# Reciprocal square roots on VectorE in 8 steps for one column and 11 for several, in place of 12

## The chip, the cores and the metric

The kernel runs on one core of one Trainium2 chip. The metric is device time in microseconds (us) of the whole program. Below, PE is TensorE (matmuls; PEld are its weight loads), DVE is VectorE, ACT is ScalarE, POOL is GpSimd, and SP is SyncE, which issues most DMAs. P is 128, the number of partitions; "128x3" is a tile of 128 partitions with 3 elements each, which the texts call 3 columns.

## The reference

One step of a diffusion backbone of width 1024 with one layer: 128 context tokens and 1024 latent tokens, nine blocks of 128. Each layer has an attention head group (8 query heads and 2 key heads of 64) and a bidirectional mLSTM head group (4 heads of 128) side by side, one output projection, and a SwiGLU FFN of hidden width 2816. What matters for this change is that a root-mean-square norm stands at five places of the layer:

```python
def rmsnorm(x, w):
    xf = x.astype(F32)
    y = xf * lax.rsqrt(jnp.mean(xf * xf, axis=-1, keepdims=True) + EPS)
    return (y * w.astype(F32)).astype(x.dtype)

def trunk_layer(x, mods, ...):
    sh1, sc1, g1, sh2, sc2, g2 = mods
    h = rmsnorm(x, norm1_w) * (1 + sc1) + sh1
    aq, ak, av, mq, mk, mv, mo, mg = jnp.split(h @ w_in, SPLIT_POINTS, axis=-1)
    aq = rmsnorm(aq.reshape(B, T, N_Q_HEADS, HEAD_DIM), q_norm_w)
    ak = rmsnorm(ak.reshape(B, T, N_KV_HEADS, HEAD_DIM), k_norm_w)
    ...
    attn_o = attention(aq, keys, vals)
    hm, st_f, st_b = mlstm_bidir(...)
    hm = rmsnorm(hm.transpose(0, 2, 1, 3), mlstm_norm_w.reshape(MLSTM_HEADS, MLSTM_DV))
    hm = (hm.reshape(B, T, MLSTM_WIDTH) * jax.nn.sigmoid(mo.astype(F32))).astype(x.dtype)
    mix = jnp.concatenate([attn_o, hm], axis=-1) @ w_out
    x = x + g1 * mix
    h2 = rmsnorm(x, norm2_w) * (1 + sc2) + sh2
    x = x + g2 * swiglu(h2, w_gu, w_down)
    return x, ak, av, st_f, st_b
```

and once more over the result (`y_prompt = rmsnorm(xp, final_norm_w)`, and the same for the samples).

## The kernel before, in words

The nine token blocks are held in three column blocks (c) of three blocks each (CB is 3, CT is 384 tokens). The program runs in these stages, by the trace's time: loads, the adaLN modulations, the norm of x and its transposes (to about 100 us); the input projection, the q and k norms with rotary and the mLSTM scans (100 to 490); the context tokens' output projection (`prefill`) beside the last mLSTM head and the first attention scores (490 to 610); attention with the output projection and the FFN of earlier column blocks woven beside it (610 to 980); the last column block's norm and the start of the seven-product FFN stage (980 to 1060); that stage's gate and up products (1060 to 1460); and the last outputs.

Products of f32 quality are made of two parts: a weight block is loaded as `raw` (or straight as `whi`), and its high part and remainder are multiplied separately. In the last FFN stage, `weights6` makes the two halves of each operand: ACT casts the scaled high part (L1637, tile A), DVE the remainder (L1638), and the PE lines L1651 to L1653 use them.

The function the change touches is `rsqrt` (L130). From a sum of squares `ss` in n columns it makes v = ss * inv + plus, a first guess of the reciprocal root out of the bits of v by integer arithmetic (a shift, L137, and a multiply and add, L138), and three Newton steps of three DVE instructions each (L140, L141, L142). Every instruction reads what the one ahead of it wrote. Its tiles are rv (v), rh (the shifted bits), ry (the guess) and rt.

It is called 23 times:

- `normalise` (L401), three times with 3 columns: ssx, the sums of squares of x that ACT made (L400), at 10, 15 and 42 us.
- `norm_rope` (L718), eight times with 2 to 16 columns: the q and k norms, between 73 and 174 us.
- the `tail` of `head_mlstm` (L980), six times: three times 9 columns (305, 412, 509 us) and three times 3 columns (519, 532, 559 us); POOL multiplies the head's output hm by the root (L981).
- `stats` (L1445), six times. Three times with one column in `end` of `prefill`, one for each block (575, 577, 583 us): ACT squares a block (L1444), and `norm2` on ACT reads the root (L1460) and goes on to transposes on PE and to the scaled result `fl` (L1470). Three times with 3 columns (721, 941, 1020 us), the last in `finish`, where DVE writes the result (L1531).

What sets the order on each engine is a scheduler: the program's tasks are given in the written order with priorities (`hot(n)` raises it for a few), and the Tile framework sets the instructions of each engine's queue by simulating the program with its own costs. One instruction fewer can so move others on every engine. Each engine runs its queue in order, and an instruction whose operand isn't ready holds up everything behind it.

Names in the other lines of the prediction: L232 sums squares of weight blocks of w_in (iraw); L488 copies the modulation strips (part) out of a PSUM bank for the PE line L497; L615 and L616 are steps of the mLSTM gates (gc, gd), each with an ACT table load; L192 to L208 make a power of two (pv) that PE spreads; L960 makes nu in the mLSTM and L957 reads sd and va; L1134 to L1139 are the softmax of attention (S, pr, ph, pl).

Of the kernel before, what the change touches and what calls it, by code (L numbers as in the profile page):

```python
# [12 lines left out]
I32 = mybir.dt.int32  # L13
AF = mybir.ActivationFunctionType
ALU = mybir.AluOpType
# [4 lines left out]
P = 128  # L20
# [30 lines left out]
def hybrid_step(ctx: ExitStack, tc: tile.TileContext, I: dict, O: dict):  # L51
# [3 lines left out]
    dve = nc.vector  # L55
# [7 lines left out]
    def nm(s):  # L63
        uid[0] += 1
        return f"{s}_{uid[0]}"
# [64 lines left out]
    def rsqrt(tp, ss, n, inv, cap=16, plus=EPS):  # L130

        v = tp.tile([P, cap], F32, name=nm("rv"), tag="rv", bufs=2)[:, :n]
        y = tp.tile([P, cap], F32, name=nm("ry"), tag="ry", bufs=2)[:, :n]
        t = tp.tile([P, cap], F32, name=nm("rt"), tag="rt", bufs=2)[:, :n]
        h = tp.tile([P, cap], I32, name=nm("rh"), tag="rh", bufs=2)[:, :n]
        dve.tensor_scalar(out=v, in0=ss, scalar1=inv, scalar2=plus, op0=ALU.mult, op1=ALU.add)
        dve.tensor_scalar(out=h, in0=v.bitcast(I32), scalar1=1, scalar2=None, op0=ALU.logical_shift_right)  # L137
        dve.tensor_scalar(out=y.bitcast(I32), in0=h, scalar1=-1, scalar2=0x5F3759DF, op0=ALU.mult, op1=ALU.add)  # L138
        for _ in range(3):
            dve.tensor_tensor(out=t, in0=y, in1=y, op=ALU.mult)  # L140
            dve.scalar_tensor_tensor(out=t, in0=t, scalar=-0.5, in1=v, op0=ALU.mult, op1=ALU.mult)  # L141
            dve.scalar_tensor_tensor(out=y, in0=t, scalar=1.5, in1=y, op0=ALU.add, op1=ALU.mult)  # L142
        return y

# [216 lines left out]
    for n in (1, 4):  # L361
        dve.tensor_scalar(out=bcol[:, n * KD : (n + 1) * KD], in0=bcol[:, n * KD : (n + 1) * KD],
                          scalar1=1.0, scalar2=None, op0=ALU.add)
# [31 lines left out]
    def normalise(c):  # L395

        ssx = p0.tile([P, CB], F32, name=f"ssx{c}")
        for i in range(CB):
            jk = p0.tile([P, D], BF16, name=nm("jk"), tag="jk", bufs=2)
            act(jk, x3[c][:, i], AF.Square, accum_out=ssx[:, i : i + 1])  # L400
        rs = rsqrt(p0, ssx, CB, 1.0 / D)  # L401
        for i in range(CB):
            dve.tensor_scalar(out=x3[c][:, i], in0=x3[c][:, i], scalar1=rs[:, i : i + 1], scalar2=None, op0=ALU.mult)
# [305 lines left out]
    def norm_rope(qp, cc, ss, x, nb, nh, w, rb):  # L709

        skip = nb - (rb[1] - rb[0])
        n = nb * nh
        sq = qp.tile([P, 1024], F32, name=nm("nr0"), tag="nr0", bufs=1)[:, 0 : n * HD].rearrange("p (h d) -> p h d", d=HD)
        xf = x.rearrange("p b h d -> p (b h) d")
        act(sq, xf, AF.Square)
        ssum = qp.tile([P, 16], F32, name=nm("nrs"), tag="nrs", bufs=2)[:, :n]
        dve.tensor_reduce(out=ssum, in_=sq, axis=AX.X, op=ALU.add)
        r = rsqrt(qp, ssum, n, 1.0 / HD)  # L718
        pool.tensor_tensor(out=xf, in0=xf, in1=bc(r, 2, [P, n, HD]), op=ALU.mult)
        if skip:  # L720
            pool.tensor_tensor(out=xf[:, 0 : skip * nh], in0=xf[:, 0 : skip * nh], in1=bc(w, 1, [P, skip * nh, HD]), op=ALU.mult)
        if rb[1] == rb[0]:
            return
        t2 = qp.tile([P, 1024], F32, name=nm("nr1"), tag="nr0", bufs=1)[:, 0 : n * HD].rearrange("p (b h d) -> p b h d", b=nb, d=HD)
        for i, b in enumerate(range(rb[0], rb[1])):
            s4 = ss[:, b, :].rearrange("p (a f) -> p a f", a=2)
            x4 = x[:, skip + i].rearrange("p h (a f) -> p h a f", a=2)
            t4 = t2[:, skip + i].rearrange("p h (a f) -> p h a f", a=2)
            for f in range(2):
                dve.tensor_tensor(  # L730
                    out=t4[:, :, :, 16 * f : 16 * f + 16],
                    in0=x4[:, :, :, 16 - 16 * f : 32 - 16 * f],
                    in1=bc(s4[:, :, 16 * f : 16 * f + 16], 1, [P, nh, 2, 16]),
                    op=ALU.mult)
        m = nb - skip
        pool.tensor_tensor(out=x[:, skip:], in0=x[:, skip:], in1=bc(cc[:, rb[0] : rb[1], :], 2, [P, m, nh, HD]), op=ALU.mult)
        dve.tensor_tensor(out=x[:, skip:], in0=x[:, skip:], in1=t2[:, skip:], op=ALU.add)
# [155 lines left out]
    def head_mlstm(h, st):  # L893
# [44 lines left out]
        for b in range(NB):  # L938
# [36 lines left out]
            if b in ends:  # L975
                def tail(b=b):
                    b0 = ends[b]
                    n = b + 1 - b0
                    v = hm[:, b0 : b + 1, :]
                    r = rsqrt(mlp, ssh[:, b0 : b + 1], n, 1.0 / P)  # L980
                    pool.tensor_tensor(out=v, in0=v, in1=bc(r, 2, [P, n, P]), op=ALU.mult)  # L981
                    for c in range(b0 // CB, b // CB + 1):
                        if c == 0:
                            dma(hm_d[0][:, h * P : (h + 1) * P].rearrange("(b p) n -> p b n", p=P), hm[:, 0:CB, :])
                        else:
                            (pool.dma_start if alone else dma)(hm_d[c][:, h], hm[:, c * CB : (c + 1) * CB, :].rearrange("p b n -> p (b n)"))

                tails.append(tail)
                if h != NH - 2:
                    tails.pop()()  # L990
# [1000 lines left out]
```

## Time and profile before

| what | value |
|---|---|
| timed runs | 1489.94, 1495.63, 1496.03 us; median 1495.63 |
| profiled execution | 1491.52 us, of which its span is 1489.8 us |
| granted TensorE clock, mean | 0.989 |
| PE, DVE, ACT, POOL busy | 1406.6, 1102.7, 875.8, 218.7 us |
| DVE instructions on the page | 2233 |
| DMA | 206.46 MB, mean 139 GB/s |

The span is the time between the first and the last instruction of the trace; the time of an execution has a little around it. A row of the timeline gives the start, the length, the engine, the line, the operation, what is written and read, and in brackets how long the engine had been idle and what ended that. A row of a group gives how many instructions there were, the shortest, median and longest in ns, the first and last start in us, and the forms. A row of waits gives the total us, the number of times, and the longest.

### The profile page before, as it was taken

What the parts mean: (1) busy time and instruction counts of PE and PEld (TensorE: products, weight loads), DVE (VectorE), ACT (ScalarE), POOL (GpSimd) and SP (SyncE); (2) the same over time, 40 slices, a digit from 0 to 9 for tenths busy, and PEclk for the clock granted to TensorE, in tenths of its full rate; (3) what the DMA queues carried; (4) which work ended last, traced back from release to release, by engine and by line L of the source; (5) the groups of instructions that cost most, each with busy time, mean ns of one, the idle gap of its engine ahead of it and who ended that gap; (6) DMA issues with size and microseconds to landing.
All of it is one profiled execution on the core that took longest, in us unless ns stands there. A gap on an engine that the chain in (4) does not pass through costs nothing.

```text
span 1489.8 us, 22801 instructions
## 1 busy us (share of the span) xinstructions
PE 1406.6 (94%) x8285; PEld 986.0 (66%) x8285; DVE 1102.7 (74%) x2233; ACT 875.8 (59%) x1619; POOL 218.7 (15%) x310
## 2 busy tenths in 40 slices
PE   6789999998899889999999999999999999999996
PEld 3634667766677657888999997985645654654552
DVE  4978556775777978667687768798976867786667
ACT  5854476866857745563766754859642642463254
POOL 0113422232222434420100010010000000000000
PEclk9999999999999989999999999999999999999998
DMA  9565323643558966675757765469231321232112
GB/s 368 174 193 197 96 75 65 145 90 74 92 108 166 198 200 163 157 212 159 212 162 167 188 138 155 142 209 348 88 105 43 112 74 43 72 116 67 45 43 85
DMA packets 256166, 206.46 MB, mean 139 GB/s; under 512 B 167022, under 2 KB 208198, under 8 KB 256054
## 3 DMA queue, kind: packets, MB, share of 16 engines
q1 hardware_dynamic: 253054, 199.00, 48.2%
q10 hardware_dynamic: 2872, 5.62, 1.2%
q8 instruction: 65, 1.06, 0.3%
q14 instruction: 47, 0.39, 0.1%
q0 software_dynamic: 128, 0.39, 0.1%
HBM read 153.38 MB, written 13.26 MB: 112 GB/s over the span
## 4 chain that ended last, share of the span: by engine, by line
PE 51%; DVE 6%; DMA 5%; ACT 4%; issue 2%; POOL 1%; SPq 0%; ACTq 0%; DVEq 0%; POOLq 0%
PE mm L1651 5%; PE mm L1653 5%; PE mm L1652 5%; PE mm L1482 3%; PE mm L1481 3%; PE mm L1483 3%; PE mm L1735 3%; PE mm L1736 3%; PE mm L1737 3%; PE mm L1220 2%; PE S L1132 2%; PE mm L1221 2%; PE mm L1222 2%; PE mm L1256 1%; PE mm L1258 1%
## 5 line engine op out<-in xcount | busy, mean ns | idle before, releaser
L1652 PE MATMUL mm<-Bt,A 128*128 128x384 f16 x616 | 200.8, 326 | 0.0
L1651 PE MATMUL mm<-Bt,A 128*128 128x384 f16 x616 | 198.4, 326 | 1.5 <-DVE u L1670 1.2
L1653 PE MATMUL mm<-Bt,A 128*128 128x384 f16 x616 | 197.4, 326 | 2.3 <-DVE A L1638 2.2
L146 DVE TENSOR_TENSOR wlo<-raw,whi 128x1024 fp32r<-128x1024 f32 (+1 forms) x78 | 95.1, 1221 | 38.6 <-ACT whi L175 35.2
L1139 DVE SCALAR_TENSOR_TENSOR pl<-pr,st,ph 128x1152 f16<-128x1152 f32 (+1 forms) x72 | 96.1, 1335 | 36.9 <-ACT ph L1138 36.9
L175 ACT CAST whi<-raw 128x1024 fp32r<-128x1024 f32 (+1 forms) x78 | 79.7, 1027 | 70.7 <-PE mm L1221 26.2
L1483 PE MATMUL mm<-aTh,wlo 128*128 128x384 f32 x352 | 119.1, 339 | 0.5 <-DVE wlo L146 0.5
L1481 PE MATMUL mm<-aTh,whi 128*128 128x384 f32 x352 | 119.2, 339 | 0.0
L1482 PE MATMUL mm<-aTl,whi 128*128 128x384 f32 x352 | 118.9, 338 | 0.0
L1135 ACT ACTIVATE pr<-S,st 128x1152 f32<-128x1152 f32 (+1 forms) x72 | 81.5, 1132 | 56.9 <-DVE st L1134 55.6
L1134 DVE TENSOR_REDUCE st<-S 128x1 f32<-128x1152 f32 (+1 forms) x72 | 88.9, 1235 | 25.4 <-PE S L1132 25.3
L530 PE MATMUL wi<-headw,hT 128*128 128x384 f16 x288 | 94.5, 328 | 1.2 <-ACT th L820 1.2
L531 PE MATMUL wi<-headw,hT 128*128 128x384 f16 x288 | 94.5, 328 | 0.0
L532 PE MATMUL wi<-headw,hT 128*128 128x384 f16 x288 | 94.3, 328 | 0.0
L1138 ACT ACTIVATE ph<-pr,st 128x1152 f16<-128x1152 f32 (+1 forms) x72 | 83.8, 1164 | 13.9 <-DVE st L1137 5.3
L1132 PE MATMUL S<-kst,qT 128*128 128x384 f32 (+1 forms) x400 | 87.6, 349 | 4.0 <-ACT pr L1135 4.0
L1653 PEld LDWEIGHTS <-A 128*128 128x128 f16 x616 | 60.3, 98 | 43.4 <-DVE A L1638 3.8
L1652 PEld LDWEIGHTS <-A 128*128 128x128 f16 x616 | 60.3, 98 | 42.0 <-issue 2.2
L1651 PEld LDWEIGHTS <-A 128*128 128x128 f16 x616 | 60.3, 98 | 40.4 <-ACT A L1637 0.4
L146 POOL TENSOR_TENSOR hl<-tn,hl 128x384 fp32r<-128x384 f32 x22 | 30.7, 1396 | 309.0 <-ACT hl L1504 285.3
L1132 PEld LDWEIGHTS S<-kst,qT 128*128 128x128 f32 x400 | 69.4, 189 | 7.8 <-ACT pr L1135 5.4
L1637 ACT ACTIVATE A<-S,six 128x1024 f16<-128x1024 f32 x44 | 48.9, 1142 | 38.7 <-DVE S L1632 19.4
(478 smaller groups left out, 3718.9 us busy)
## 6 DMA issues: line engine op xcount, KB each, us to landing
raw<-in_w_gu_dram SPq DMA_DIRECT2D x88, 512.0 KB, 3.4
raw<-in_w_down_dram SPq DMA_DIRECT2D x42, 512.0 KB, 3.8
a<-in_w_ada_dram SPq DMA_DIRECT2D x24, 512.0 KB, 6.5
whi<-in_w_down_dram SPq DMA_DIRECT2D x22, 512.0 KB, 8.7
iraw<-in_w_in_dram SPq DMA_DIRECT2D x32, 256.0 KB, 3.4
x<-in_x_sample_dram SPq DMA_DIRECT2D x11, 512.0 KB, 5.9
raw<-in_w_out_dram SPq DMA_DIRECT2D x10, 512.0 KB, 3.7
aw<-in_w_ada_dram SPq DMA_DIRECT2D x8, 512.0 KB, 6.0
```

Source lines behind the costliest of these rows:

```text
L146: (dve if eng == "dve" else pool).tensor_tensor(out=out, in0=full, in1=hi, op=ALU.subtract)
L530: mm(ps[:, :n], ah, wh[:, k % 2, c0 : c0 + n], start=(k == 0), stop=False)
L531: mm(ps[:, :n], ah, wl[:, k % 2, c0 : c0 + n], start=False, stop=False)
L532: mm(ps[:, :n], al, wh[:, k % 2, c0 : c0 + n], start=False, stop=(k == KD - 1))
L1132: mm(S[:, n, 0:w], qT[:, h, :], kst[kv][:, t, c0 + n * w : c0 + (n + 1) * w], start=(t == 0), stop=(t == 1))
L1139: dve.scalar_tensor_tensor(out=plv, in0=prv, scalar=st[:, 3:4], in1=phv, op0=ALU.mult, op1=ALU.subtract)
L1481: mm(ps, wh[:, k, :], th[:, k, :], start=(k == 0), stop=False)
L1482: mm(ps, wh[:, k, :], tl[:, k, :], start=False, stop=False)
L1483: mm(ps, wl[:, k, :], th[:, k, :], start=False, stop=(k == KD - 1))
L1651: mm(ps, wh[:, k], bt[:, 0, k], start=first and k == 0, stop=False, skip_group_check=True)
L1652: mm(ps, wh[:, k], bt[:, 1, k], start=False, stop=False, skip_group_check=True)
L1653: mm(ps, wl[:, k], bt[:, 0, k], start=False, stop=k == 3, skip_group_check=True)
```

## The change

Two things are done with `rsqrt`. First, v is kept as -v/2: the factor -0.5 goes into the scale and the addend of the first instruction, so no later step needs it, and the first guess is made from the bits of that in one instruction in place of two. The bits of -v/2 read as an integer, times -0.5 and plus a constant, are the guess; the tile rh goes. That makes 11 instructions out of 12. Second, for a single column the two multiplications y * y * v of a Newton step are one instruction, in which y stands as the per-column scalar operand: 8 instructions out of 12. For several columns the second multiplication is a plain one of two tensors.

```diff
         t = tp.tile([P, cap], F32, name=nm("rt"), tag="rt", bufs=2)[:, :n]
-        h = tp.tile([P, cap], I32, name=nm("rh"), tag="rh", bufs=2)[:, :n]
-        dve.tensor_scalar(out=v, in0=ss, scalar1=inv, scalar2=plus, op0=ALU.mult, op1=ALU.add)
-        dve.tensor_scalar(out=h, in0=v.bitcast(I32), scalar1=1, scalar2=None, op0=ALU.logical_shift_right)
-        dve.tensor_scalar(out=y.bitcast(I32), in0=h, scalar1=-1, scalar2=0x5F3759DF, op0=ALU.mult, op1=ALU.add)
+        dve.tensor_scalar(out=v, in0=ss, scalar1=-0.5 * inv, scalar2=-0.5 * plus, op0=ALU.mult, op1=ALU.add)
+        dve.tensor_scalar(out=y.bitcast(I32), in0=v.bitcast(I32), scalar1=-0.5, scalar2=0x5F3759DF - 2 ** 30 - 2 ** 22, op0=ALU.mult, op1=ALU.add)
         for _ in range(3):
-            dve.tensor_tensor(out=t, in0=y, in1=y, op=ALU.mult)
-            dve.scalar_tensor_tensor(out=t, in0=t, scalar=-0.5, in1=v, op0=ALU.mult, op1=ALU.mult)
+            if n == 1:
+                dve.scalar_tensor_tensor(out=t, in0=y, scalar=y, in1=v, op0=ALU.mult, op1=ALU.mult)
+            else:
+                dve.tensor_tensor(out=t, in0=y, in1=y, op=ALU.mult)
+                dve.tensor_tensor(out=t, in0=t, in1=v, op=ALU.mult)
             dve.scalar_tensor_tensor(out=y, in0=t, scalar=1.5, in1=y, op0=ALU.add, op1=ALU.mult)
         return y
```

PE, ACT, POOL and SP have as many instructions as before, but the scheduler puts some of them in another order. In the changed kernel lines from 143 on have a number one higher. Three places follow; rows are an instruction's line, operation, and what it writes and reads.

ACT where the mLSTM gates' steps (gc, gd) meet the modulation strips (part), at 96 to 102 us of the trace; before:

```order
L232 ACTIVATE jkw,isc_1224<-iraw_1073 128x512
L615 ACT_TABLE_LOAD
L615 ACTIVATE gc<-gb 128x128
L232 ACTIVATE jkw,isc_1224<-iraw_1073 128x512
L488 COPY part_1190<-mm_962 128x512
L616 ACT_TABLE_LOAD
L616 ACTIVATE gd<-gc 128x128
L775 ACTIVATE qraw_1310<-wi_1084,isc_736 128x512
```

and now:

```order
L233 ACTIVATE jkw,isc_1214<-iraw_1067 128x512
L616 ACT_TABLE_LOAD
L616 ACTIVATE gc<-gb 128x128
L233 ACTIVATE jkw,isc_1214<-iraw_1067 128x512
L617 ACT_TABLE_LOAD
L617 ACTIVATE gd<-gc 128x128
L489 COPY part_1182<-mm_956 128x512
L776 ACTIVATE qraw_1298<-wi_1078,isc_730 128x512
```

The copy to part now stands behind the second table load and gd.

DVE in `end` of `prefill`, at the single-column calls (574 to 584 us); before:

```order
L136 TENSOR_SCALAR rv_7074<-s_1414_7071 128x1
L137 TENSOR_SCALAR rh_7077<-rv_7074 128x1
L138 TENSOR_SCALAR ry_7075<-rh_7077 128x1
L140 TENSOR_TENSOR rt_7076<-ry_7075 128x1
L1134 TENSOR_REDUCE st_7191<-S_7192 128x1
L141 SCALAR_TENSOR_TENSOR rt_7076<-rt_7076,rv_7074 128x1
L1209 TENSOR_TENSOR t_1434_7173<-mm_7160,gl_6966 128x512
L136 TENSOR_SCALAR rv_7143<-s_1427_7140 128x1
L142 SCALAR_TENSOR_TENSOR ry_7075<-rt_7076,ry_7075 128x1
L146 TENSOR_TENSOR mx_7176<-mm_7177,mx_7176 128x512
```

and now:

```order
L135 TENSOR_SCALAR rv_7040<-s_1397_7037 128x1
L136 TENSOR_SCALAR ry_7041<-rv_7040 128x1
L139 SCALAR_TENSOR_TENSOR rt_7042<-ry_7041,rv_7040 128x1
L143 SCALAR_TENSOR_TENSOR ry_7041<-rt_7042,ry_7041 128x1
L147 TENSOR_TENSOR mx_7132<-mm_7133,mx_7132 128x512
```

The softmax's reduction (L1134) and the gating of the next block (L1209), which stood between the first call's steps, now stand behind its first Newton step, and the remainder mx (L146), which stood last here, directly follows that step.

ACT at the start of the last FFN stage (1012 to 1018 us): the squares of the last norm (L1444) and the casts of A (L1637); before:

```order
L1444 ACTIVATE jk_11524,s_2272_11523<-x1a 128x1024
L1637 ACTIVATE A_11492<-S_11484,six 128x2x512
L1637 ACTIVATE A_11495<-S_11484,six 128x2x512
L1444 ACTIVATE jk_11526,s_2272_11523<-x1a 128x1024
L1637 ACTIVATE A_11498<-raw_11482,six 128x512
L1444 ACTIVATE jk_11528,s_2272_11523<-x1a 128x1024
```

and now:

```order
L1445 ACTIVATE jk_11471,s_2250_11470<-x1a 128x1024
L1445 ACTIVATE jk_11473,s_2250_11470<-x1a 128x1024
L1638 ACTIVATE A_11439<-S_11431,six 128x2x512
L1638 ACTIVATE A_11442<-S_11431,six 128x2x512
L1445 ACTIVATE jk_11475,s_2250_11470<-x1a 128x1024
L1638 ACTIVATE A_11445<-raw_11429,six 128x512
```

The second square moved ahead of the two casts. On SP, nearby, loads of w_gu (`raw`) and of w_down (`whi`) change places.

## The prediction

> **What bounds the kernel now.** I read the page first (busy time, then the chain that ended last), then a table of stages, then the waits of TensorE (PE) in the stages where it idles. Section 1 and the first line of section 4 of the page:
>
> ```profile
> PE 1406.6 (94%) x8285; PEld 986.0 (66%) x8285; DVE 1102.7 (74%) x2233; ACT 875.8 (59%) x1619; POOL 218.7 (15%) x310
> ...
> PE 51%; DVE 6%; DMA 5%; ACT 4%; issue 2%; POOL 1%; SPq 0%; ACTq 0%; DVEq 0%; POOLq 0%
> ```
>
> PE is busy 1406.6 us of a span of 1489.8, so everything that is not matmul can give back at most 83 us. VectorE (DVE), on which the change lies, holds 6% of the chain. Where PE idles is told by stage (columns: stretch, its length, then busy us and instructions of PE, PEld, DVE, ACT, POOL, the granted clock, the DMA share, GB/s):
>
> ```profile
> 0.00:100.00 100.00, 73.39 (x520) 46.28 (x521) 70.66 (x244) 66.01 (x145) 12.54 (x19) 0.97 0.77 255
> 100.00:490.00 390.00, 373.93 (x2457) 257.71 (x2458) 273.00 (x706) 258.30 (x636) 114.00 (x213) 0.99 0.51 115
> 490.00:610.00 120.00, 101.99 (x577) 78.47 (x577) 99.03 (x258) 69.22 (x151) 50.63 (x50) 0.96 0.65 171
> 610.00:980.00 370.00, 365.26 (x2012) 330.95 (x2011) 274.11 (x409) 238.57 (x353) 38.56 (x28) 1.00 0.64 171
> 980.00:1060.00 80.00, 76.48 (x430) 48.28 (x430) 71.49 (x123) 59.00 (x94) 2.98 (x1) 1.00 0.73 260
> 1060.00:1460.00 400.00, 399.73 (x2224) 217.41 (x2222) 290.47 (x430) 170.36 (x209) 0.00 (x0) 1.00 0.22 72
> ```
>
> From 1060 to 1460 PE idles 0.27 us: nothing on DVE pays there. What can pay lies in the front (26.6 us idle to 100), in 490 to 610 (18.0), and in 980 to 1060 (3.5). The 16.1 us of 100 to 490 are spread over 390.
>
> **The change part by part.** First, how many steps go. The first integer step ran once per call, 23 times:
>
> ```profile
> L137 DVE TENSOR_SCALAR rh<-rv x23: 142/170/2109, 10.5 to 1021.6; 128x3 int32<-128x3 int32 x9, 128x16 int32<-128x16 int32 x4, 128x8 int32<-128x8 int32 x3, 128x9 int32<-128x9 int32 x3
> ```
>
> The 19 forms listed all have several columns; of the four not listed, one has two columns (the first of eight calls of norm_rope) and three have one (stats in prefill's end). So 20 calls lose one step and three lose four: 32 instructions. What a step is worth depends on what stands behind it (start, length):
>
> ```profile
> 11.45 0.16 DVE L140 TENSOR_TENSOR rt<-ry 128x3 f32<-128x3 f32 x1
> 11.64 0.16 DVE L141 SCALAR_TENSOR_TENSOR rt<-rt,rv 128x3 f32<-128x3 f32 x1
> 11.72 0.20 DVE L351 COPY bcol<-mm 128x48 f32<-128x48 f32 x1
> 11.92 0.15 DVE L142 SCALAR_TENSOR_TENSOR ry<-rt,ry 128x3 f32<-128x3 f32 x1
> ```
>
> L141 reads what L140 wrote and starts 0.19 us after it; the copy at 11.72, which needs neither, starts 0.08 after L141. A step on the path is thus worth 0.195 us, one whose gap other work fills some 0.07. The change holds 32 x 0.07 = 2.2 us of DVE throughput, and 32 x 0.195 = 6.2 us if every step is on the path that ends last. That is the scale: at most 0.4% of the time.
>
> The Trainium skill, in "VectorE: DVE Perf Modes", The DRAIN you can't avoid, has a DVE instruction wait until the pipe of the one before is empty, with the semaphore costing nothing extra. By it an independent step would cost its whole 0.16 us too, and the bound on throughput would be 32 x 0.16 = 5.1 us in place of 2.2; the copy at 11.72, begun inside L141's 0.16 us, disagrees, and I go by the row.
>
> *Front, three calls at 10, 15 and 42 us: 0.* The third is the only one near PE's idle time:
>
> ```profile
> 41.13 1.06 ACT L400 ACTIVATE jk<-x 128x1024 bf16<-128x1024 f32 x1 [0.73 <-DMA x<-in_x_sample_dram]
> 42.31 0.17 DVE L136 TENSOR_SCALAR rv<-ssx 128x3 f32<-128x3 f32 x1 [1.26 <-ACT jk L400]
> 42.39 0.13 DVE L192 TENSOR_SCALAR pv<-pv 1x1 f32<-1x1 f32 x1
> 43.05 0.37 PE L208 MATMUL mm<-pv,one 1*128 1x2 f32 x1 [2.31 <-DVE pv L195]
> ```
>
> PE waits for pv, which is queued behind rv, and rv waits for a transfer of x. The step removed follows rv, and pv's steps already run in its gap. Whatever the normalised rows win before 96 us is given back to the next transfer that ScalarE (ACT) waits 3.08 us for, the first line here:
>
> ```profile
> 96.47 0.63 ACT L232 ACTIVATE jkw<-iraw 128x512 bf16<-128x512 f32 x1 [3.08 <-DMA iraw<-in_w_in_dram]
> 97.21 1.28 ACT L615 ACT_TABLE_LOAD   x1
> 99.34 0.56 ACT L488 COPY part<-mm 128x512 f32<-128x512 f32 x1
> 99.92 1.28 ACT L616 ACT_TABLE_LOAD   x1
> 99.95 1.02 PE L497 MATMUL mm<-part,strip_sel 128*2 128x512 f32 x2 [2.11 <-ACT part L488]
> 101.21 0.31 ACT L616 ACTIVATE gd<-gc 128x128 f32<-128x128 f32 x1
> ```
>
> The cover is that transfer; were it gone, the front's three steps would give 3 x 0.195 = 0.6.
>
> *ACT's order at 97 to 102 us: +1.5.* In the new order the table load (1.28) and gd (0.31) stand ahead of the copy to part: 1.59 us later for part, for which PE already waited 2.11 with nothing else to run. Queued behind it are qraw and ACT's evacuations. Bounds: 0 if part's matmuls move behind other work that is ready, 1.6 if PE only waits longer; as PE had nothing ready at 97.8, I take 1.5. The 32 fewer steps don't do this; the scheduler's new order does.
>
> *Normalising of the mLSTM heads, 305 to 560 us: -0.3.* Where GpSimd (POOL) runs a tensor operation, an integer step can sit out its whole length:
>
> ```profile
> 518.89 2.12 POOL L981 TENSOR_TENSOR hm<-hm,ry 128x1152 f32<-128x1152 f32 x1 [0.31 <-DVE rv L136]
> 518.92 2.11 DVE L137 TENSOR_SCALAR rh<-rv 128x3 int32<-128x3 int32 x1
> 522.43 0.71 PE L957 MATMUL wi<-va,sd 128*128 128x129 f32 x4 [1.50 <-DVE nu L960]
> ```
>
> Nu, for which PE waits 1.50 us, stood in DVE's queue behind that step. The step left in its place has the same operand kinds and may sit out the same 2.1 us, so the gain lies between 1.5 (it no longer meets L981) and -0.6 (it meets it a step earlier, for a like stall of some 2.1 where PE has only 1.5 in hand). One dependent step, and a little for the others, is 0.3.
>
> *The three single-column calls, 574 to 584 us: -0.4.* Four steps fewer each, 0.8 us in a row, and other work between:
>
> ```profile
> 579.55 1.29 POOL L1210 TENSOR_TENSOR x1a<-x1a,t 128x512 f32<-128x512 f32 x1 [0.95 <-DVE rt L140]
> 579.58 1.27 DVE L141 SCALAR_TENSOR_TENSOR rt<-rt,rv 128x1 f32<-128x1 f32 x1
> 580.93 1.04 ACT L1444 ACTIVATE jk<-x1a 128x1024 bf16<-128x1024 f32 x1
> 581.97 1.32 ACT L1460 ACTIVATE t<-x1a,ry 128x512 f32<-128x512 f32 x2
> 586.51 1.17 PE L1256 MATMUL mm<-whi,mx 128*128 128x512 f32 x4 [2.08 <-DVE fl L1470]
> ```
>
> A step with two tensors sat 1.27 us beside GpSimd's 1.29. The roots' reader is L1460 on ACT, queued directly behind a square (L1444) of 1.04 us that doesn't wait for any root; then come transposes, L1470 and PE. So the gain is cut to what ACT's queue passes on. Upper bound: PE's whole wait for L1470, 2.08 us. Lower: the three new steps read a per-column operand, and the nearest row of such a read is
>
> ```profile
> L1752 DVE TENSOR_SCALAR lq<-st x6: 206/214/215, 1461.9 to 1483.6; 128x1 f32<-128x1 f32 x6
> ```
>
> 0.214 against 0.15 to 0.16 for the steps above, 0.06 more; nine of them make 0.5 us lost if nothing else is passed on. I take a half step per removed one at one call, 4 x 0.195 / 2 = 0.4.
>
> *ACT and SP at 1010 to 1024 us: +0.5.* In the new order a second square (L1444) stands ahead of the two casts of A:
>
> ```profile
> 1012.76 1.04 ACT L1444 ACTIVATE jk<-x1a 128x1024 bf16<-128x1024 f32 x1
> 1013.80 2.17 ACT L1637 ACTIVATE A<-S,six 128x1024 f16<-128x1024 f32 x2
> 1014.96 2.48 DVE L1638 SCALAR_TENSOR_TENSOR A<-S,six,A 128x1024 f16<-128x1024 f32 x2 [3.67 <-ACT A L1637]
> ...
> PE mm L1653 <- DVE A L1638: 2.2, 3, 1.1
> ```
>
> The casts come 1.04 later (1.23 with the 0.19 that reads the sum), and PE waited 2.2 us for their remainders already. Bounds 0 (matmuls of the pair before still fill it) and 1.2; I take 0.5. SP's loads change order too, with the DMA share at 0.73; at nothing here, and a rival below.
>
> *The rest: 0.* The q and k norms between 73 and 174 us and the calls at 720 and 941 lie beside PE work (3.3% and less idle from 610 to 980); uncovered, their 10 steps are 2.0 us.
>
> Sum: 0 + 1.5 - 0.3 - 0.4 + 0.5 + 0 = +1.3 us. The profiled run took 1491.52 (span 1489.8 and 1.7 around it), so 1492.8. The three timed runs are 1489.94, 1495.63 and 1496.03 (median 1495.63): the profiled one lies near their fastest, and with it the four have a mean of 1493.3. The shift on that mean is 1494.6; I say **1494.5**.
>
> **The rivals.** About 0.5%, 7.5 us, is what a measurement of this kernel can tell from no change.
>
> *Every step on the path* (12%): 1493.3 - 6.2 = 1487, and with the L1470 and nu waits gone as well (2.1 + 1.5) 1483.5. For it: every step waits for the one before, and DVE is 89% busy in 980 to 1060 (71.5 of 80). Against it: DVE's 6% of the chain, and the roots' readers stand behind ACT's queue or a transfer.
>
> *Late weights* (13%): slower. In the new order of SP's queue, loads of w_gu and w_down change places in the stage from 980 to 1060, where the DMA share is 0.73.
>
> ```profile
> raw<-in_w_gu_dram SPq DMA_DIRECT2D x88, 512.0 KB, 3.4
> ...
> whi<-in_w_down_dram SPq DMA_DIRECT2D x22, 512.0 KB, 8.7
> ```
>
> A w_gu block behind one w_down load comes 3.4 to 8.7 us later. From the point where that passes the slack ahead of L1637, PE stands still for it, since each pair's products need its A: 1493.3 + 1.3 + 8.7 = 1503.3 at the full price, 1498 at the lower. Against it: with that share PE idles only 3.5 of these 80 us, and none of the waits there is for a transfer of w_gu.
>
> *The order gives nothing and takes nothing* (part of my own case's chance): part's matmuls fill other gaps and the rest cancels: 1493.3, within 0.5%. That the change doesn't do what it says, 12 steps still, gives the same.
>
> **How the numbers follow.** My forecast with the absorbed case has 75%, its own range 1490 to 1498. All steps on the path have 12%, late weights 13%. Only the full prices of the rivals leave the band of 0.5% around 1495.63 (1488.2 to 1503.1), so half of each counts: 6% faster, 6.5% slower. The order moves on every engine, so effects beyond my list are likely and of either sign; they take 9% to the fast side, where the fastest run shown, 1489.9, is already near the band's end, and 3.5% to the slow side. Faster 0.15, same 0.75, slower 0.10. Range 1486 to 1502.5: all but the extremes of either rival, and the bounds (+1.6 + 0.6 + 0.5 + 1.2 up, 0 - 1.5 - 2.1 - 0.6 - 2.0 down from 1493.3) lie inside.
>
> **What would show it.** DVE's count falls by 32, to 2201 in the profile's counting, and its busy time by 4 to 8 us (stalls included). PE's wait for part grows from 2.11 to 3.6. The wait for L1470 shrinks by under 1 us; the stall beside L981 moves to the new integer step. The 1060 to 1460 stretch stays at 400 us. I am wrong if PE's idle time of a stage falls by over 3 us, or if a wait for raw or whi appears in 980 to 1060.

## The result

The change made the kernel slower by half a per cent: 1499.05 us in the median of 17 runs (1496.83 to 1503.89), against 1491.06 us for 17 runs of the kernel before (1489.40 to 1496.99). The ratio is 1.0052 with a 95% interval of 1.0043 to 1.0061. The forecast was "no change" at 1494.5, a sum of +1.3 us on a base of 1493.3. Measured, the change costs 8.0 us, six times that sum. The time lies in the range that I gave, which was as wide as it was for the rivals' sake; that says nothing for the sum.

The page of the changed kernel, busy time and the head of the chain:

```profile
PE 1411.4 (94%) x8285; PEld 990.3 (66%) x8285; DVE 1097.0 (73%) x2201; ACT 875.1 (58%) x1619; POOL 227.1 (15%) x310
...
PE 48%; DVE 8%; ACT 5%; DMA 5%; issue 2%; POOL 0%; SPq 0%; ACTq 0%; DVEq 0%; POOLq 0%
```

DVE did what the change says: 32 instructions fewer (2233 to 2201) and 5.7 us less busy. PE ran the same 8285 matmuls, but was busy 4.8 us longer (1406.6 to 1411.4). The span grew by 7.3 us (1489.8 to 1497.1), so PE's idle time grew by only 2.5. The same matmuls were busy longer, and the granted clock was lower in two places. One is the first 100 us, with PE busy 73.39 us at a clock of 0.97 before and 76.09 at 0.90 after. This is not what makes the difference: the kernel before has 76.14 us at 0.93 there in a second profile, which took 1490.26 us. The other place is 500 to 610 us. Before (columns as in the prediction: PE, PEld, DVE, ACT, POOL busy, granted clock, DMA share, GB/s):

```profile
500.00:550.00 50.00, 40.73 (x245) 29.58 (x244) 40.49 (x109) 25.77 (x67) 17.14 (x19) 0.90 0.67 173
550.00:610.00 60.00, 54.20 (x297) 43.52 (x295) 49.06 (x130) 34.16 (x60) 27.60 (x22) 1.00 0.57 166
```

and after:

```profile
500.00:550.00 50.00, 39.36 (x230) 28.42 (x231) 37.40 (x104) 25.37 (x67) 16.27 (x17) 0.83 0.64 170
550.00:610.00 60.00, 53.32 (x286) 43.03 (x285) 43.66 (x108) 31.36 (x58) 27.09 (x21) 0.97 0.58 158
```

In these 110 us PE got 26 matmuls fewer done, and its granted clock fell from 0.90 to 0.83 and from 1.00 to 0.97. As the two kernels reach a given matmul at different times, it is surer to follow the same 601 matmuls: they took 122.02 us before (from 484.08 us, 104.01 of them busy) and 127.72 after (from 485.29, 107.10 busy). So 5.7 of the 7.3 us were lost here, 3.1 by slower matmuls and 2.6 by longer waits.

A single gap shows what a slower PE looks like. Before the change:

```profile
508.39 1.07 PE L386 MATMUL mm<-ip,gta 128*32 128x256 f32 x16 [2.58 <-DVE sd L924]
509.39 0.71 PE L957 MATMUL wi<-va,sd 128*128 128x129 f32 x4
```

and after it (lines one higher):

```profile
511.47 1.83 PE L387 MATMUL mm<-ip,gta 128*32 128x256 f32 x16 [2.59 <-DVE sd L925]
513.24 1.23 PE L958 MATMUL wi<-va,sd 128*128 128x129 f32 x4
```

The wait is the same, 2.58 and 2.59 us, for the same operand. But behind it the 16 products took 1.83 us in place of 1.07 and the next four 1.23 in place of 0.71: PE ran at half its clock in one execution and not in the other. It isn't the change that decides this. In the second profile of the kernel before, the products behind the same gap are slow too:

```profile
508.53 1.93 PE L386 MATMUL mm<-ip,gta 128*32 128x256 f32 x16 [2.96 <-DVE sd L924]
```

What decides is how the gap falls. In every trace here the granted clock changes only on a grid of slots of 3.41 us, which lies at another offset in each execution. Two slots around this gap before (columns: stretch, its length, PE busy, granted clock, DMA share, GB/s):

```profile
503.71:507.13 3.42, 2.09 (x16) 1.00 0.20 41
507.13:510.54 3.41, 2.15 (x26) 1.00 0.74 140
```

and after:

```profile
508.24:511.65 3.41, 0.82 (x10) 1.00 0.45 87
511.65:515.07 3.42, 3.42 (x24) 0.50 0.83 190
```

Before, the gap is split over two slots, in which PE idles 39% and 37%; after, it falls into one, in which PE idles 76%, and the next slot runs at half clock. In all 18 traces together, between 100 and 1470 us, each of the 43 full-clock slots in which PE idled 60% or more was followed by half clock, 21 of 38 with 50 to 60% were, and 4 of 7044 with less. So a longer gap makes half clock behind it more likely, and where the grid lies is chance. This bears on the Trainium skill ("TensorE: Matmul & The Clock Gate", What's actually happening): there an activity monitor halves the clock after an idle window of some 3.4 us, and its windows run freely. The traces agree with the length of the window and with its running freely; where the page asks for an idle window, 60% of one was enough here.

PE's waits in the stretch from 484 to 612 us, after (line, what it waited for, total us, times, longest):

```profile
PE mm L1257 <- ACT mx L1303: 2.8, 1, 2.8
PE mm L387 <- DVE sd L925: 2.6, 1, 2.6
PE wi L951 <- ACT it L954: 2.2, 1, 2.2
PE mm L125 <- ACT t L1461: 2.2, 2, 1.8
...
PE mm L498 <- ACT hmx L489: 1.5, 1, 1.5
...
PE mm L1257 <- DVE fl L1471: 1.1, 1, 1.1
```

The same waits before were 1.9 (mx), 2.6 (sd), 1.7 (it), 1.0 (t), 0.5 (hmx) and 2.3 (fl). The prediction's wait for fl shrank as it should; the waits for mx, it, t and hmx, for which its sum has no term, grew by 3.6 us together. Only t reads a root directly; the others stand behind other work in the queues. On GpSimd, before:

```profile
516.69 0.46 POOL L974 TENSOR_TENSOR hm<-hm,so 128x128 f32<-128x128 f32 x1 [4.93 <-ACT jkh L973]
517.10 1.48 POOL L1398 TENSOR_TENSOR x1a<-x1a,gta 128x512 f32<-128x512 f32 x1
518.89 2.12 POOL L981 TENSOR_TENSOR hm<-hm,ry 128x1152 f32<-128x1152 f32 x1 [0.31 <-DVE rv L136]
```

and after:

```profile
520.24 2.38 POOL L1399 TENSOR_TENSOR x1a<-x1a,gta 128x512 f32<-128x512 f32 x1 [5.40 <-DVE gta L1398]
523.33 2.12 POOL L982 TENSOR_TENSOR hm<-hm,ry 128x1152 f32<-128x1152 f32 x1 [0.71 <-DVE ry L143]
525.40 0.87 POOL L975 TENSOR_TENSOR hm<-hm,so 128x128 f32<-128x128 f32 x2
```

The gated add and the long product of hm with its root now stand ahead of the short product of the running head (L975), where one of these stood first before. On ScalarE the two products `it` and `dt` moved ahead of the squares of hm, the copy hmx behind a later square, and, at 558 us, both casts of weights behind the head's last product (L971) and its square (L974) ahead of mx. ScalarE before:

```profile
552.49 1.05 ACT L175 CAST whi<-raw 128x1024 fp32r<-128x1024 f32 x1 [0.70 <-DMA raw<-in_w_out_dram]
553.44 0.40 ACT L970 ACTIVATE hm<-nu,dn 128x128 f32<-128x128 f32 x1
553.83 1.04 ACT L175 CAST whi<-raw 128x1024 fp32r<-128x1024 f32 x1
554.78 1.07 ACT L1302 CAST mx<-mm 128x512 fp32r<-128x512 f32 x2
```

and after:

```profile
558.24 0.40 ACT L971 ACTIVATE hm<-nu,dn 128x128 f32<-128x128 f32 x1 [1.41 <-DVE dn L969]
558.54 1.03 ACT L176 CAST whi<-raw 128x1024 fp32r<-128x1024 f32 x1
559.48 1.04 ACT L176 CAST whi<-raw 128x1024 fp32r<-128x1024 f32 x1
560.43 0.30 ACT L974 ACTIVATE jkh<-hm 128x128 bf16<-128x128 f32 x1
560.73 1.05 ACT L1303 CAST mx<-mm 128x512 fp32r<-128x512 f32 x2
```

and PE, which waits for mx:

```profile
561.34 1.20 PE L1257 MATMUL mm<-whi,mx 128*128 128x512 f32 x4 [2.76 <-ACT mx L1303]
562.38 1.51 PE L1259 MATMUL mm<-wlo,mx 128*128 128x512 f32 x4
563.68 1.91 PE L1257 MATMUL mm<-whi,mx 128*128 128x512 f32 x4
565.39 1.49 PE L1259 MATMUL mm<-wlo,mx 128*128 128x512 f32 x4
```

Before, PE waited 1.87 us for mx, and each group of four behind the first took 1.07. Here the second to the fourth took 1.51, 1.91 and 1.49: the longer gap cost 0.9 us of waiting and then, by the starts of the groups, some 1.6 us of slow matmuls.

### The profile page after: what moved, and what is told of

It reads as the page before. It is cut to its first block, busy times and chain, and to the rows that moved or that the text cites. A ratio compares the mean times of both kernels' runs of the same rounds, so it can differ in the third digit from the quotient of the medians.

```text
span 1497.1 us, 22768 instructions
## 1 busy us (share of the span) xinstructions
PE 1411.4 (94%) x8285; PEld 990.3 (66%) x8285; DVE 1097.0 (73%) x2201; ACT 875.1 (58%) x1619; POOL 227.1 (15%) x310
## 4 chain that ended last, share of the span: by engine, by line
PE 48%; DVE 8%; ACT 5%; DMA 5%; issue 2%; POOL 0%; SPq 0%; ACTq 0%; DVEq 0%; POOLq 0%
PE mm L1652 4%; PE mm L1654 4%; PE mm L1653 4%; PE mm L1482 3%; PE mm L1483 3%; PE mm L1484 3%; PE mm L1736 3%; PE mm L1737 3%; PE mm L1738 3%; DMA raw<-in_w_down_dram 2%; PE S L1133 2%; PE mm L1257 2%; PE mm L1221 2%; PE mm L1222 2%; PE mm L1259 2%
## 5 line engine op out<-in xcount | busy, mean ns | idle before, releaser
L1140 DVE SCALAR_TENSOR_TENSOR pl<-pr,st,ph 128x1152 f16<-128x1152 f32 (+1 forms) x72 | 99.4, 1381 | 38.4 <-ACT ph L1139 37.4
L147 POOL TENSOR_TENSOR hl<-tn,hl 128x384 fp32r<-128x384 f32 x22 | 35.3, 1604 | 303.8 <-ACT hl L1505 281.8
```

The lines of the kernel that those rows point to most:

```text
L147: (dve if eng == "dve" else pool).tensor_tensor(out=out, in0=full, in1=hi, op=ALU.subtract)
L1140: dve.scalar_tensor_tensor(out=plv, in0=prv, scalar=st[:, 3:4], in1=phv, op0=ALU.mult, op1=ALU.subtract)
```

## The experiments

All ratios are to runs of the kernel before on the same chip, with 95% intervals. To separate steps from order, the queues were held: a table in the kernel names each engine's instructions in the wanted order, and each is chained to the one ahead of it by an edge that fixes the order of issue and adds no wait. No run holds the kernel before in its own order; that the edges cost nothing is read from the kernels held in the old order throughout or nearly so, which are no slower than before (0.998 and 0.9993).

```diff
+def pin(tc):
+    traced = list(tc.nc.cur_bb.bb.instructions)
+    for steps in ORDER:                      # one list for each engine
+        last = None
+        for at in steps:
+            if last is not None:
+                tc.add_manual_dep(traced[at], last.name, NoSync, reason="pin")
+            last = traced[at]
...
         hybrid_step(tc, ins, outs)
+        pin(tc)
```

### Steps and order, each alone

New steps in the old order (where the old order has the shift, or the square of a single column, there is nothing):

> The changed rsqrt (11 and 8 steps), with every engine's queue held in the order that the kernel before has (issue order only, no further wait). If the 8 us come from the scheduler's new order, this runs like the kernel before or up to 2.2 us faster (the throughput of 32 steps at 0.07 us): ratio 0.998 to 1.000, granted clock as before, 0.989. If they come from the new steps themselves (the per-column operand, the stalls beside GpSimd), it runs like the changed kernel: ratio 1.004 to 1.006.

Measured: 0.998 (0.9963 to 0.9996), median 1488.97 us. The profile's clock is 0.985 and not the 0.989 expected: its first 100 us have 0.90.

Old steps in the new order (the extra step stands directly ahead of its successor):

> The rsqrt of before (12 steps), with every engine's queue held in the order that the changed kernel has. If the new order costs the 8 us: ratio 1.005 to 1.007 and a granted clock of 0.98. If the new steps cost them: ratio 0.999 to 1.001 and a clock of 0.989.

Measured: 1.0071 (1.0054 to 1.0088), median 1503.1 us, clock 0.979. Both kernels were profiled once more on the same chip:

> The changed kernel once more, for another profiled execution. If its lost time is TensorE at half clock behind gaps between 490 and 570 us, the granted clock is again 0.98 and most of the half-rate windows lie in that stretch again, whatever their exact places; ratio 1.005. If the half-rate windows of the first profile were chance, they are gone here and the ratio is still 1.005.

> The kernel before once more, for another profiled execution: if the clock is a matter of the order, it is again near 0.989, with about 24 us at half rate inside the span; if it is chance, it lies anywhere between 0.98 and 0.99.

Measured: the changed kernel 1.0061 (1.0048 to 1.0074), clock 0.980; the kernel before 1490.26 us, clock 0.987. The changed kernel's second profile has in the two stretches

```profile
500.00:550.00 50.00, 40.02 (x246) 29.25 (x245) 39.39 (x110) 27.21 (x72) 17.56 (x19) 0.90 0.71 179
550.00:610.00 60.00, 53.73 (x281) 43.14 (x280) 44.79 (x109) 31.67 (x58) 27.10 (x21) 0.94 0.57 160
```

where before's second has 0.93 and 1.00. So the places of half clock move from one execution to the next (0.83 and 0.97 in the first profile), and 500 to 550 us alone does not tell the two kernels apart. I had expected most of the changed kernel's half clock between 490 and 570 us again; of 51 us at half clock in this profile up to 1475 us, 17 lie between 490 and 610, and 20 in the first 100. Over the whole span the clock is 0.982 and 0.980, against 0.989 and 0.987 before. More profiles, below, show what of this goes with the order. The four cells are:

| | old order | new order |
|---|---|---|
| 12 steps | 1 | 1.0071 |
| 11 and 8 steps | 0.998 | 1.0061 |

Read down, the steps save 0.2% (3.0 us, interval 0.6 to 5.5) in the old order, and 0.1% in the new one, where the two intervals overlap. Read across, the order costs 0.7 to 0.8% (10.6 us with the old steps, 12.1 with the new) whatever the steps. The changed kernel is slow by its order alone. What the removed instructions gave fits the 2.2 us of 32 x 0.07; the interval doesn't exclude the 5.1 of whole instructions either.

In the old order with the new steps the clock from 500 us on is again that of before (from 490 to 500 it is 0.83, against 1.00):

```profile
500.00:550.00 50.00, 42.11 (x251) 30.49 (x251) 39.83 (x109) 26.22 (x70) 18.37 (x20) 0.90 0.67 179
550.00:610.00 60.00, 54.90 (x298) 44.50 (x297) 48.17 (x116) 34.68 (x60) 28.45 (x23) 1.00 0.55 163
```

### Which part of the order

The next four have the new steps, and take the new order in one stretch of time only (or everywhere but there).

> The changed rsqrt; every queue held in the old order, except that the instructions up to 430 us stand in the new one. The theory that the new order costs its 11 us place by place: this part costs 2 to 4 us over the kernel with the new steps in the old order (0.998), by the offset of TensorE between the new and the old order at 460 us; ratio 0.999 to 1.001. The rival that the cost is spread by chance over half-rate windows, wherever the order differs: any of the three parts gives 0.998 to 1.006.

Measured: 1.0012 (0.9999 to 1.0025).

> The changed rsqrt, old order, except the stretch from 486 to 620 us in the new one: 18 instructions moved on ScalarE, 6 on GpSimd, 4 on SyncE, 28 on TensorE, 111 on VectorE. If this stretch carries the cost (the mLSTM head's tail, the context tokens' output projection and its norm): 6 to 7 us over 0.998, ratio 1.002 to 1.003, and half-rate windows between 500 and 600 us. The prediction named other places (97 and 1013 us); if it was right in that, 0.998.

Measured: 1.0059 (1.0046 to 1.0071), median 1499.37 us.

> The changed rsqrt, old order, except from 690 to 1075 us the new one, with the second square ahead of the casts of A and the exchanged loads. The offsets of TensorE there differ by about 1 us: ratio 0.998 to 0.999. The prediction's late weights: 1.001 to 1.006.

Measured: 0.9999 (0.9989 to 1.0009).

> The changed kernel's order throughout, except that the stretch from 486 to 620 us stands in the old order. If that stretch carries 6 to 7 us of the 11: ratio 1.001 to 1.002, faster than the changed kernel (1.006). If the cost is elsewhere: 1.005 to 1.006.

Measured: 1.001 (0.9996 to 1.0023).

The stretch from 486 to 620 us alone is as slow as the whole change, and without it the new order is within 0.1% of before. Taken out of the changed kernel (1.0061) it gives back 0.0051, 7.6 us; put into the old order (0.998) it costs 0.0079, 11.8 us. I had expected 6 to 7 either way. The three parts do not add up: over 0.998 they cost 0.0032, 0.0079 and 0.0019, 0.0130 together, where the whole costs 0.0081. The base of 0.998 has an interval of 0.0033, which can account for much of the difference, since it enters three times on one side and once on the other; whether the rest is delay of one stretch absorbed in the next is open. That one part carries most of the cost both ways speaks against a cost spread by chance wherever the order differs. The two places to which the prediction gave a cost lie in the two parts that cost less, 97 us in the first (a part of 4.8 us, where I had expected 2 to 4) and 1013 us in the third (2.8).

The profiles say the same. The 601 matmuls from 484 to 606 us, followed through the kernels of this section and the others (us; the kernels with fillings, told of below, aside):

| order in this stretch | profiles | time, mean | PE busy, mean | PE idle, mean | granted clock, 490 to 610 us |
|---|---|---|---|---|---|
| old, or old but for GpSimd | 8 | 117.3 to 122.0, 119.4 | 102.9 | 16.6 | 0.94 to 0.99 |
| new in one half of it (below) | 2 | 124.6 and 124.6 | 106.3 | 18.3 | 0.93 |
| new | 5 | 125.2 to 129.1, 127.3 | 106.7 | 20.6 | 0.91 to 0.93 |

The first and the last row do not overlap. The order costs 7.9 us here, half of it in slower matmuls (3.9) and half in longer waits (4.0).

### Inside that stretch

> The changed rsqrt, old order, except from 486 to 538 us the new one (GpSimd's six, 8 on ScalarE, 8 on TensorE, 50 on VectorE). By the offset of TensorE at 530 us this costs 2.7 us, and half a half-rate window more or less: ratio 0.999 to 1.001.

Measured: 1.0016 (1.0004 to 1.0028).

> The changed rsqrt, old order, except from 545 to 620 us the new one: the casts of weights ahead of the head's last squares and of mx on ScalarE, and the single-column calls. By the offsets between 550 and 590 us this costs 3 to 4 us, of which about 1.7 is one half-rate window behind the wait for mx: ratio 1.000 to 1.001.

Measured: 1.002 (1.0007 to 1.0034).

> The changed rsqrt, old order on all engines but GpSimd, whose six instructions between 500 and 535 us stand in the new order: the 2.12 us product of hm and the root (L982) and a gated add (L1399) ahead of the 0.46 us products of the head that is still running (L975). If the root that is ready a step earlier does its harm by this: 2 to 3 us over 0.998, ratio 0.999 to 1.000. If ScalarE's order does it: 0.998.

Measured: 0.9993 (0.9982 to 1.0005).

Both halves count, 5.4 and 6.0 us over 0.998, each more than I expected. GpSimd's six instructions by themselves make 1.9 us, a bit under the 2 to 3 expected, but the intervals of 0.9993 and 0.998 overlap, and in its profile the 601 matmuls took 118.8 us, no longer than in the old order: that GpSimd's order alone costs something is not shown. Which of the engines' orders does, or which of them together, was not tried.

### Half clock or the waits themselves

The first try put small matmuls, whose results are not used, into free columns of PSUM banks in the longest gaps:

```diff
+    def warm(out, k):
+        for _ in range(k):
+            mm(out, ident, ident[:, 0:120], start=True, stop=True)
...
+                if alone and b in FILL_M:
+                    warm(pm[:, 392:512], FILL_M[b])
```

> The changed kernel in its own order, with 80 small matmuls on TensorE that compute nothing that is used, put into the five longest gaps of the stretch (ahead of the strips at 511 us, the two products at 528 and 530, the row at 534 and the first output product at 561). If TensorE at half clock behind these gaps is a good part of the loss, the half-rate windows between 500 and 570 us go (17 us after 500 us in the changed kernel's first profile) and 4 to 6 us with them: ratio 1.002 to 1.003. If only the waits count, the ratio stays at 1.005 to 1.006 or rises by what the small matmuls delay.

Measured: 1.0097 (1.0076 to 1.0119), slower by 5 to 7 us than without them (1.0052 and 1.0061). The clock did what was expected:

```profile
500.00:550.00 50.00, 42.36 (x328) 34.60 (x329) 35.22 (x99) 23.08 (x62) 14.51 (x17) 1.00 0.58 162
550.00:610.00 60.00, 56.38 (x330) 46.42 (x328) 43.93 (x109) 30.00 (x55) 26.96 (x21) 1.00 0.56 161
```

It is 1.00 throughout, but the page counts 8445 matmuls, two for each f32 one put in, and the twenty in the first gap took 4.62 us where the gap is 2.6, so the head's own products came later. The second try cut them to the gaps' lengths:

> The changed kernel in its own order, with 37 small matmuls whose results are not used (10, 8, 3, 5 and 11, each 0.22 us in the run before) in the same five gaps, now no longer than the gaps. If the half clock behind the gaps costs 4 to 5 us of the changed kernel's 8: no half-rate window between 500 and 570 us and a ratio of 1.002 to 1.003. If the gaps alone count, or the small matmuls cost what they save: 1.005 to 1.007.

Measured: 1.0032 (1.0020 to 1.0044), median 1497.38 us, profile clock 0.989:

```profile
500.00:550.00 50.00, 42.70 (x303) 33.06 (x302) 40.63 (x114) 28.78 (x75) 17.71 (x21) 1.00 0.75 183
550.00:610.00 60.00, 55.57 (x316) 45.77 (x315) 46.84 (x114) 32.58 (x60) 28.45 (x23) 1.00 0.54 161
```

The first gap there, filled, and the products behind it:

```profile
508.49 2.39 PE L130 MATMUL mm<-ident 128*128 128x120 f32 x20
511.62 1.07 PE L392 MATMUL mm<-ip,gta 128*32 128x256 f32 x16 [0.73 <-DVE sd L932]
```

The 16 products take 1.07 us again. With the order unchanged, and more work on PE, 0.0020 to 0.0029 are gone (against 1.0052, whose interval this one just touches, and 1.0061, of which it is clear), 3.0 to 4.3 us. So half clock behind the gaps is about that part of the loss, in line with the 3.9 us by which the same matmuls are busy longer in the new order. What is left, 1.0032, would be the longer waits (4.0 us); no run took these away alone. The same in the old order:

> The changed rsqrt in the old order (0.998), with 23 such matmuls (9, 6, 1 and 7) in four gaps of that order. If half clock counts: the windows at 508 and 525 us go, 2 to 4 us with them, ratio 0.9955 to 0.997. If not: 0.998 to 1.000.

Measured: 0.9991 (0.9978 to 1.0003), not better than 0.998. Its clock:

```profile
500.00:550.00 50.00, 43.52 (x291) 33.62 (x292) 41.98 (x108) 27.44 (x73) 16.49 (x19) 0.97 0.70 178
550.00:610.00 60.00, 55.68 (x301) 44.99 (x301) 47.06 (x114) 33.55 (x59) 27.42 (x22) 0.97 0.55 161
```

Against 0.90 and 1.00 without the filling, it rose in the first stretch and fell in the second. The 2 to 4 us that I expected did not come; what the filling itself cost there was not told apart. That filling pays is shown for the new order only.

### Which part of the change

```diff
+        if n == 1:
+            (the new steps)
+        else:
+            (the old steps)
```

> 8 steps for one column, 12 for several, in the order that the scheduler gives: it is the order of before but for a few instructions (none on GpSimd and SyncE, 2 rows on ScalarE). If the order decides: as before or a little faster, 0.998 to 1.001. If the per-column operand costs: 1.001 or more.

Measured: 0.9991 (0.9979 to 1.0002).

> 11 steps for several columns, 12 for one, in the order that the scheduler gives: it is the changed kernel's order on ScalarE, GpSimd and SyncE to the row, and but for 3 rows on TensorE. If the order decides: like the changed kernel, 1.004 to 1.007, with 20 of the 32 instructions gone. If it was the single-column steps: 0.998 to 1.000.

Measured: 1.0067 (1.0051 to 1.0083), median 1501.07 us.

This was foreseen from the orders alone. With the steps cut for one column, the scheduler gives every engine the old order but for a few rows, none of them on GpSimd (the short product of the head at 518.09 us, then the gated add at 518.51 and the long product at 520.28), and the time is that of before. With one step less for several columns, it gives the new order, on GpSimd to the row (the gated add at 517.69, the long product at 520.78, and then two short ones at 522.85).

The single step saved in 20 chains, which is worth some tenths of a per cent at most, tipped the scheduler into the order that costs 0.7%. By what rule inside it the root that comes a step earlier moves the others stays open.

Of all kernels run, the new steps in the old order have the lowest ratio, 0.998 (1488.97 us): faster than before and than the change, though not clear of the 0.9991 to 0.9999 of four others.

## Why the prediction was wrong, by its own steps

- **What bounds the kernel.** Right as to stages: 1060 to 1460 us lasts as long as before, and the loss lies in the stretches where PE idled. It read only PE's idle time as what can change, though, and took busy time as given. Of the 7.9 us that the order costs from 484 to 606 us, 3.9 are busy time.
- **What a step is worth, 0.07 to 0.195 us.** Not contradicted. The steps alone gave 3.0 us (0.6 to 5.5), between the 2.2 of throughput and the 6.2 of every step on the path. My sum had 0.7 for them, since I counted PE's waits one by one. The section of the Trainium skill that I cited ("VectorE: DVE Perf Modes", The DRAIN you can't avoid) also lets an instruction that isn't held start earlier, so the row of the copy need not disagree with it; I read the rule too widely.
- **The per-column operand, +0.06 us.** Right in size, and too small to matter: the nine new steps (L139) took 219 ns in the median, 209 at the least.
- **ACT's order at 97 us, +1.5.** The copy to part did come behind the table load and gd, 1.16 us later (99.34 to 100.50), but PE was late too: its last product ahead of this wait started at 98.29 us in place of 97.47. So the wait grew from 2.1 to 2.5 rather than to 3.6:

```profile
100.50 0.57 ACT L489 COPY part<-mm 128x512 f32<-128x512 f32 x1
```

```profile
PE mm L498 <- ACT part L489: 2.5, 1, 2.5
```

- **The heads' normalising, -0.3, and the order elsewhere, 0.** This is the step that failed. The sum priced the new order at two places, 97 and 1010 us, and put what it moves anywhere else at nothing. For the heads it asked only whether the integer step would still sit out GpSimd's long product. In the trace the step ahead of it sat out most of it (1.63 us), where L137 had sat out 2.11; that was within its bounds:

```profile
523.84 1.63 DVE L135 TENSOR_SCALAR rv<-ssh 128x3 f32<-128x3 f32 x1
```

 What it left out is that the queues of all engines changed here, between 486 and 620 us, GpSimd's in a few rows only. That stretch of the order costs 7.6 to 11.8 us by the runs and 7.9 by the profiles.
- **The single-column calls, -0.4.** Right in sign, by the first pair of profiles: from the four products L1260 at 569.85 us to the transposes at 606.59, behind all three calls, PE took 36.74 us before and 36.04 after. The waits moved from fl (2.3 to 1.1, a little more than the 1 us that I allowed) to t (1.0 to 2.2). The calls alone measured 0.9991 (0.9979 to 1.0002), which is not clear of nothing.
- **ACT and SP at 1010 us, +0.5, and the rival of late weights.** The order from 690 to 1075 us costs 0.0019 over 0.998, 2.8 us with an interval that reaches to zero. PE's waits for the remainders of A there fell, from 2.2 to 1.6, and no wait for a load of w_gu appeared. The rival ended on the right side and named the wrong mechanism.

```profile
PE mm L1654 <- DVE A L1639: 1.6, 2, 1.4
```

- **The sum.** It added places, each with its own wait, and had no term for what a longer gap does to the clock behind it. It also gave the order's unlisted effects 9% to the fast side and 3.5% to the slow side, with no other ground than how near the band's end the fastest run lay; the order was the largest effect. The base of 1493.3 was 2.2 us above the 1491.06 that 17 runs gave, which brought the forecast nearer to the time by luck. PE's idle share from 610 to 980 us, put at 3.3% and less, reaches 3.6% (900 to 980), which changes nothing.

## What to carry to other kernels

Where a scheduler sets the order, an edit of a few instructions is two changes, the edit and the order it tips, and the second can be the larger; hold the old order with the new code, and the new order with the old code, and the two can be read apart. In a stretch where TensorE idles in short gaps, count what a longer gap costs twice: the wait itself, and the matmuls behind it at half clock. Read every engine's queue in such a stretch, and give a price to what the order moves there even where no single row looks costly: here that was the largest effect, and no one engine's share of it could be named.

## What was not expected of the hardware

- A gap of 2.6 us was enough for TensorE to run at half clock behind it in some executions (the 16 products of L387 in 1.83 us) and not in others (1.07 us). On the grid of 3.41 us, a slot at full clock with PE idle 60% or more was always followed by half clock (43 of 43). Of the slots at half clock, one with PE idle under 10% was always followed by full clock (69 of 69), one with 20% or more never (none of 23).
- The runs of one kernel spread over 7 us (1489.4 to 1497.0 before, 1496.8 to 1503.9 after), and part of the spread goes with the granted clock: of 98 runs of the kernel before beside the experiments, the 17 with a clock of 0.989 or more have a median of 1490.1 us, the 23 with 0.983 or less 1493.1.
- Three dozen small matmuls whose results nobody reads made a kernel 3 to 4 us faster; twice as many made it 5 to 7 us slower.
